# Second norm's rstd in two steps, another PSUM set for a bias product, later token blocks in a fused transformer block

## The chip, the cores and the metric

The kernel runs on one core of a Trainium2 chip. The core has a matrix engine (TensorE, PE in the profile), three engines for elementwise work (VectorE or DVE, ScalarE or ACT, GpSimd or POOL), a queue that issues transfers (SyncE or SP) and 16 DMA engines. Each engine takes its own instructions in the order in which they stand in its queue, and waits for others only where a semaphore says so. The metric is the time of one execution on the device, in microseconds (us).

## The reference

One residual layer on 512 tokens of width 2048, all in float32: a modulated norm, a projection shared by a recurrent and an attention group, an output projection, and then the part in which the change lies, a second modulated norm and a SwiGLU feed-forward of width 5632.

```python
x = x + gt1[:, None, :] * (mix @ w_out[l])

h2 = modulate(rms_norm(x, g_ffn[l]), sh2, sc2)
gate, up = jnp.split(h2 @ w_up[l], 2, axis=-1)
x = x + gt2[:, None, :] * ((jax.nn.silu(gate) * up) @ w_down[l])
```

`rms_norm` divides by the root of the mean square (rstd is its inverse) and multiplies by a gain; `modulate` multiplies by one plus a scale and adds a shift.

## The kernel before

Every product is made of three: each operand is split into a high part (written by ScalarE) and the low rest (written by VectorE), and high x high, high x low and low x high are summed in PSUM. A contraction of 2048 runs over 16 steps of 128 (k-steps). Activations lie transposed: features on partitions, 512 tokens along the free axis.

Weights come in raw pieces of 1 MB (tag `raw`, two buffers), and `stream` (from L188) splits each in two halves of 1024 columns (tags `whi` and `wlo`, three buffers each; L181 is the high part on ScalarE, L182 the low part on VectorE). One half serves two k-steps. `fm_group` (L201 on) computes four output blocks of 128 features at once, in four PSUM banks, 12 matmuls per k-step, and runs the functions in `hooks` after the k-steps that they are booked for.

The feed-forward goes in three stages:
- **Plain up groups** (`for gi in range(STD)`, L876 on): two groups, up0 and up1, of 16 k-steps. Their input `hr` is x times the gain of the norm, without rstd, since rstd of a token can be multiplied in later. The shift goes in as a bias product: `up_bias` sums shift x weight on VectorE into `bu_acc`, in 16 instructions, and a product with ones (`bup_p`, L886 to L888) adds it over the partitions; L889 copies it to `bup`. L892 to L895 then apply rstd, bias and SiLU.
- **Token side of the fast blocks.** For the other blocks of the up projection a Strassen-like scheme of seven half-size products is used. `make_t(j)`, j = 0 to 7, prepares its token-side operands from a pair of feature blocks: rstd and gain (`h2x`, L824), shift (L825), sums and differences (`ta`, `tb`) and splits (`tb`, `tc`, `td`, `te` with h and l). It is VectorE and ScalarE work and runs as hooks of up0 and up1: j = 0 to 3 after the k-steps 6, 9, 12, 15 of up0, j = 4 to 7 after the k-steps 0, 3, 6, 9 of up1. From j = 2 on its results go to pages (`t_tags`) that hold `hr` until up1 has used it, so they wait for k-steps of up1.
- **Fast blocks** uf4 to uf43 (from L931), and then the **down projection**: dn0 to dn3 in two passes.

rstd itself is made by `rstd_bcast`, booked after k-step 4 of up0 (`R1STEP`): four small matmuls add the squares (`rstd_1a`), VectorE copies four columns (`rstd_1t`), GpSimd raises to the power -1/2 (L232, L235), four matmuls spread the result over the partitions (`rstd_1b`), ScalarE copies it out.

PSUM has eight banks in two sets: `acc` is one set of four; `misc` (three) with `rgp` (one) is the other. `bank(i, f, name)` gives set `acc` for even i and the other for odd i. up0 has `acc`, up1 the other set; fast block f takes `bank(f + 1, ...)`, and down group g of pass pi `bank(g + pi, ...)`. A bank is free for the next user when its last reader has read it.

The order of each queue is set by a scheduler from the priority of each piece of code (its place in the program, moved by `high_priority`), within what data and buffers allow.

Of the kernel before, what the change touches and what calls it, by code (L numbers as in the profile page):

```python
# [60 lines left out]
def block_kernel(ctx, tc, xT, crow, adaT, vecs, bfr, w1, wyr, wqkv0, wqkv, wgate, wout, wup0, wups, wdown, outT):  # L61
# [19 lines left out]
    def misc(name):  # L81
        return psm.tile([P, S], F32, tag="misc", name=name, bufs=3)

    def rgp(name):
# [151 lines left out]
        if inv is not None:  # L236
            nc.gpsimd.tensor_mul(inv, inv, out)

    def rstd_bcast(ssq, n, name, inv=None, times=None):
        ps = rgp(name + "a")  # L240
        for t in range(NT):
            nc.tensor.matmul(ps[:, t:t + 1], lhsT=ssq[:, t * P:(t + 1) * P], rhs=ones[:, 0:1], start=True, stop=True)
        tok = small(NT, name + "t")
        nc.vector.tensor_copy(out=tok, in_=ps[:, :NT])
        rms_rstd(tok, tok, n, inv)
        if times is not None:
            nc.gpsimd.tensor_mul(tok, tok, times)
        pb = rgp(name + "b")
        for t in range(NT):
            nc.tensor.matmul(pb[:, t * P:(t + 1) * P], lhsT=tok[:, t:t + 1].broadcast_to([P, P]), rhs=ident,  # L250
                             start=True, stop=True)
        out = cp.tile([P, S], F32, name=name, tag="rstd_b", bufs=2)
        nc.scalar.activation(out, pb, AF.Copy)
        return out
# [496 lines left out]
    def bank(i, f, name):  # L751
        return acc(name) if i % 2 == 0 else (misc(name) if f < 3 else rgp(name))
# [120 lines left out]
        nc.sync.dma_start(out=d[1], in_=lo)  # L873
        actd.append(d)

    for gi in range(STD):  # L876
        hk = {}
        if gi == 0:
            add(hk, R1STEP, lambda: r1.append(rstd_bcast(ssq_1, D, "rstd_1")))
        for j in range(gi * 4, gi * 4 + 4):  # L880
# [1 line left out]
        bu_acc = cp.tile([P, S], F32, name=f"bu_acc{gi}", tag="rstd_b", bufs=2)
        bup = cp.tile([P, 4], F32, name=f"bup{gi}")
        ps = fm_group(wup0[gi], list(range(KT)), hr, f"up{gi}", hooks=hk, raw_hook=lambda q, raw: up_bias(q, raw, bu_acc),
                      ps=[bank(gi, f, f"up{gi}p{f}") for f in range(4)])
# [1 line left out]
        for f in range(4):
            nc.tensor.matmul(pb[:, f:f + 1], lhsT=bu_acc[:, f * P:(f + 1) * P], rhs=ones[:, 0:1], start=True, stop=True)  # L888
        nc.vector.tensor_copy(out=bup, in_=pb[:, :4])  # L889
        for f in range(2):  # L890
# [176 lines left out]
```

## Time and profile before

| | us |
|---|---|
| median of 3 runs | 2217.01 (2216.24 to 2224.03) |
| the profiled execution | 2219.23 |
| its span, first to last instruction | 2217.5 |
| PE busy in the span | 2114.4 (95%) |
| DVE busy | 1589.6 (72%) |
| ACT busy | 879.1 (40%) |
| mean granted TensorE clock | 0.981 of full |

The profile is of one execution. A timeline row gives the start, the duration, the engine, the line, and in square brackets how long the engine was idle before and what ended that. Durations of instructions that follow each other overlap a little, so work is summed from start to start where a stretch is full. The granted clock 1.0 is the level 2.4 GHz, 0.5 the level 1.2 GHz.

### The profile page before, as it was taken

Reading aid. Unit: us, or ns where it says so; the run is one execution under the profiler, and the core shown is the slowest. Engines: PE = TensorE matmul, PEld = TensorE weight load, DVE = VectorE, ACT = ScalarE, POOL = GpSimd, SP = SyncE. Lnnn points to the kernel's source line nnn. Section 1 sums busy time; section 2 is a strip of 40 time slices with the busy share of each in tenths; the row PEclk is TensorE's granted clock in tenths of the full one; section 3 lists DMA queues with packets and bytes.
Section 4 is the critical chain, followed back from the end, with each engine's and each line's share of the span. In section 5 each row is a group of like instructions: output and inputs, shape, how many; then the busy total and the mean of one; then the engine's idle time right before and its main releaser. Section 6 shows DMA issues by size and latency. Waiting matters only on the chain.

```text
span 2217.5 us, 32702 instructions
## 1 busy us (share of the span) xinstructions
PE 2114.4 (95%) x12785; PEld 1917.1 (86%) x12785; DVE 1589.6 (72%) x2407; ACT 879.1 (40%) x1238; POOL 217.8 (10%) x169
## 2 busy tenths in 40 slices
PE   8988988898989989899999999999999999999999
PEld 5768887887778878799999999999999888888887
DVE  8997678878877777988888888888888343322332
ACT  5522336657443334544444444444444222222111
POOL 2260113333112400000000000000000000000000
PEclk9999999999999999999999999999999999999999
DMA  9868565565657762343444344433444985554443
GB/s 315 319 208 294 190 230 195 194 235 190 233 179 268 261 221 77 114 133 125 128 139 133 125 128 140 133 125 128 139 133 139 325 296 192 175 199 140 158 156 110
DMA packets 133021, 406.05 MB, mean 183 GB/s; under 512 B 14561, under 2 KB 19841, under 8 KB 123138
## 3 DMA queue, kind: packets, MB, share of 16 engines
q1 hardware_dynamic: 132866, 403.96, 54.1%
q8 instruction: 100, 1.64, 0.3%
q14 instruction: 55, 0.45, 0.1%
HBM read 361.15 MB, written 42.75 MB: 182 GB/s over the span
## 4 chain that ended last, share of the span: by engine, by line
PE 66%; DVE 14%; DMA 12%; issue 4%; ACT 3%; POOL 1%; SPq 0%; POOLq 0%; DVEq 0%; ACTq 0%
PE dn_0p L186 5%; PE dn_3p L186 5%; PE dn_1p L186 5%; PE dn_2p L186 5%; DMA ada<-in_adaT 4%; DMA bw<-in_w 2%; DVE adf L143 2%; DVE ada L133 1%; PE up0p L186 1%; DVE ada L143 1%; PE yr1p L186 1%; DMA xrl<-xrd 1%; DMA adf<-in_adaT 1%; PE up1p L186 1%; PE uf42p L941 1%
## 5 line engine op out<-in xcount | busy, mean ns | idle before, releaser
L133 DVE SCALAR_TENSOR_TENSOR ada<-ada,c_b 128x1024 f32<-128x1024 f32 x128 | 167.3, 1319 | 53.5 <-DMA ada<-in_adaT 53.4
L182 DVE TENSOR_TENSOR uq_0tl<-uq_0r,uq_0th 128x1024 fp32r<-128x1024 f32 x40 | 49.0, 1225 | 63.6 <-ACT uq_0th L181 63.6
L181 ACT ACTIVATE uq_0sh<-uq_0r 128x1024 fp32r<-128x1024 f32 x40 | 42.5, 1062 | 89.5 <-PE uf5p L941 2.3
L182 DVE TENSOR_TENSOR uq_0al<-uq_0r,uq_0ah 128x1024 fp32r<-128x1024 f32 x40 | 49.0, 1225 | 40.0 <-ACT uq_0ah L181 40.0
L181 ACT ACTIVATE uq_1th<-uq_1ra 128x1024 fp32r<-128x1024 f32 x40 | 42.5, 1061 | 73.0 <-DVE uq_1ra L921 3.0
L181 ACT ACTIVATE uq_0th<-uq_0r 128x1024 fp32r<-128x1024 f32 x40 | 42.4, 1060 | 72.4 <-DVE uq_0r L921 1.9
L181 ACT ACTIVATE uq_1sh<-uq_1rb 128x1024 fp32r<-128x1024 f32 x40 | 42.5, 1062 | 70.3 <-PE uf43p L941 2.4
L181 ACT ACTIVATE uq_1ah<-uq_1ra 128x1024 fp32r<-128x1024 f32 x40 | 42.5, 1062 | 60.7 <-issue 59.1
L181 ACT ACTIVATE uq_0ah<-uq_0r 128x1024 fp32r<-128x1024 f32 x40 | 42.4, 1060 | 51.7 <-issue 48.1
L143 DVE SCALAR_TENSOR_TENSOR adf<-adf,c_b 128x1024 f32<-128x1024 f32 x32 | 56.5, 1765 | 2.7 <-DMA adf<-in_adaT 2.7
L182 DVE TENSOR_TENSOR uq_1tl<-uq_1ra,uq_1th 128x1024 fp32r<-128x1024 f32 x40 | 49.0, 1226 | 10.5 <-ACT uq_1th L181 10.4
L186 PE MATMUL w1p<-hph,w1h 128*128 128x512 f32 x128 | 48.3, 405 | 7.7 <-ACT hph L315 7.6
L186 PE MATMUL w1p<-hpl,w1h 128*128 128x512 f32 x128 | 51.7, 404 | 2.3 <-DVE hpl L316 2.2
L182 DVE TENSOR_TENSOR uq_0sl<-uq_0r,uq_0sh 128x1024 fp32r<-128x1024 f32 x40 | 49.0, 1226 | 3.7
L182 DVE TENSOR_TENSOR uq_1sl<-uq_1rb,uq_1sh 128x1024 fp32r<-128x1024 f32 x40 | 49.0, 1226 | 2.7 <-ACT uq_1sh L181 0.6
L186 PE MATMUL w1p<-hph,w1l 128*128 128x512 f32 x128 | 50.5, 394 | 0.0
L182 DVE TENSOR_TENSOR uq_1al<-uq_1ra,uq_1ah 128x1024 fp32r<-128x1024 f32 x40 | 48.6, 1215 | 0.1
L562 DVE SCALAR_TENSOR_TENSOR ba<-bw,sh,ba 128x512 f32<-128x512 f32 x45 | 33.5, 756 | 19.4 <-DMA bw<-in_w 17.0
L143 DVE SCALAR_TENSOR_TENSOR ada<-ada,c_b 128x1024 f32<-128x1024 f32 x32 | 41.2, 1288 | 3.6 <-DMA ada<-in_adaT 3.6
L182 DVE TENSOR_TENSOR dn_1l<-dn_2r,dn_1h 128x1024 fp32r<-128x1024 f32 x11 | 13.5, 1226 | 38.2 <-ACT dn_1h L181 38.2
L182 DVE TENSOR_TENSOR dn_0l<-dn_2r,dn_0h 128x1024 fp32r<-128x1024 f32 x11 | 13.5, 1225 | 37.6 <-ACT dn_0h L181 37.6
L182 DVE TENSOR_TENSOR dn_1l<-dn_0r,dn_1h 128x1024 fp32r<-128x1024 f32 x11 | 13.5, 1225 | 37.0 <-ACT dn_1h L181 37.0
(13854 smaller groups left out, 8429.3 us busy)
## 6 DMA issues: line engine op xcount, KB each, us to landing
ada<-in_adaT SPq DMA_DIRECT2D x160, 512.0 KB, 5.1
uq_0r<-in_wups SPq DMA_DIRECT2D x80, 512.0 KB, 4.1
uq_1ra<-in_wups SPq DMA_DIRECT2D x40, 512.0 KB, 4.0
uq_1rb<-in_wups SPq DMA_DIRECT2D x40, 512.0 KB, 3.3
adf<-in_adaT SPq DMA_DIRECT2D x32, 512.0 KB, 5.4
actd<-ach SPq DMA_DIRECT2D x44, 256.0 KB, 2.1
actd<-acl SPq DMA_DIRECT2D x44, 256.0 KB, 4.0
dn_0r<-in_wdown SPq DMA_DIRECT2D x11, 1024.0 KB, 5.0
```

The source lines that it names most:

```text
L133: nc.vector.scalar_tensor_tensor(out=t, in0=t, scalar=1.0, in1=cs, op0=ALU.mult, op1=ALU.mult, accum_out=ac)
L143: nc.vector.scalar_tensor_tensor(out=t, in0=t, scalar=1.0, in1=c_b[:, cs], op0=ALU.mult, op1=ALU.mult, accum_out=ada_acc[j][:, hf, i:i + 1])
L181: nc.scalar.activation(R(hi[:, :n]), raw_ap, AF.Copy)
L182: tail_lo.append(nc.vector.tensor_sub(R(lo[:, :n]), raw_ap, hi[:, :n]).ins)
L186: nc.tensor.matmul(ps, lhsT=R(l), rhs=R(r), start=start, stop=stop)
L562: nc.vector.scalar_tensor_tensor(out=ba[j], in0=src, scalar=s1, in1=ba[j], op0=ALU.mult, op1=ALU.add)
L941: nc.tensor.matmul(m[p], lhsT=R(w[:, ks]), rhs=R(x), start=first and p in opens, stop=last, skip_group_check=True)
```

## The change

Four things. (1) `rstd_bcast` is cut into `sums` and `spread`: for the second norm the sums are booked after k-step 7 of up0 and the spreading after k-step 9, in place of both after k-step 4. (2) `make_t` is booked after the k-steps 10, 11, 13, 15 of up0 and 0, 4, 9, 15 of up1 (`T_STEPS`). (3) The bias product of up1 goes to a bank of set `acc`, and its copy gets a higher priority; up0's stays in `misc`. (4) The fast block f takes `bank(f, ...)` in place of `bank(f + 1, ...)`, so that uf4 has `acc` and uf43 the other set. The number of instructions is the same.

```diff
-R1STEP = 4
+R1STEP = (7, 9)
+T_STEPS = ((10, 11, 13, 15), (0, 4, 9, 15))
...
-    def rstd_bcast(ssq, n, name, inv=None, times=None):
-        ps = rgp(name + "a")
+    def rstd_parts(ssq, n, name, inv=None, times=None):
+
         tok = small(NT, name + "t")
...
+        def sums():
+            ps = rgp(name + "a")
...
+        def spread():
+            pb = rgp(name + "b")
...
+    def up_fin(gi, ps, bu_acc):
+        bup = cp.tile([P, 4], F32, name=f"bup{gi}")
+        pb = acc(f"bup_p{gi}") if gi % 2 else misc(f"bup_p{gi}")
+        for f in range(4):
+            nc.tensor.matmul(pb[:, f:f + 1], lhsT=bu_acc[:, f * P:(f + 1) * P], rhs=ones[:, 0:1], start=True, stop=True)
+        with tc.high_priority(offset=600):
+            nc.vector.tensor_copy(out=bup, in_=pb[:, :4])
+        up_out(gi, ps, bup, range(2))
...
-            add(hk, R1STEP, lambda: r1.append(rstd_bcast(ssq_1, D, "rstd_1")))
-        for j in range(gi * 4, gi * 4 + 4):
-            add(hk, (R1STEP + 2 if gi == 0 else 0) + (j % 4) * 3, lambda j=j: make_t(j))
+            r1_sums, r1_spread = rstd_parts(ssq_1, D, "rstd_1")
+            add(hk, R1STEP[0], r1_sums)
+            add(hk, R1STEP[1], lambda: r1.append(r1_spread()))
+        for j in range(4):
+            add(hk, T_STEPS[gi][j], lambda j=j + 4 * gi: make_t(j))
...
-        pb = misc(f"bup_p{gi}")
...
-        ps = [bank(f + 1, b, f"uf{f}p{b}") for b in range(4)]
+        ps = [bank(f, b, f"uf{f}p{b}") for b in range(4)]
```

What this does to the queues stands in the order of the built programs, at three places. First PE in up0, around the rstd of the second norm. Before, at the end of k-step 4:

```order
L186 MATMUL up0p_7046<-hrh_6969,up_0l 128x512
L242 MATMUL rstd_1a<-ones,ssq_5686 128x1 x4
L186 MATMUL up0p_7043<-hrh_6973,up_0h 128x512
L186 MATMUL up0p_7043<-hrl_6974,up_0h 128x512
L186 MATMUL up0p_7043<-hrh_6973,up_0l 128x512
L250 MATMUL rstd_1b<-ident,rstd_1t 128x128 x4
L186 MATMUL up0p_7044<-hrh_6973,up_0h 128x512
```

After, at the end of k-step 7, with 24 matmuls of two k-steps between the two products:

```order
L187 MATMUL up0p_7046<-hrh_6981,up_1l 128x512
L247 MATMUL rstd_1a<-ones,ssq_5686 128x1 x4
L187 MATMUL up0p_7043<-hrh_6985,up_0h 128x512
...
L187 MATMUL up0p_7046<-hrh_6989,up_0l 128x512
L256 MATMUL rstd_1b<-ident,rstd_1t 128x128 x4
L187 MATMUL up0p_7043<-hrh_6993,up_1h 128x512
```

So the spreading stands 24 matmuls behind the sums, where it stood three behind. Next DVE at the same place, where `rstd_1t` is the copy between the two products and `up0r` a raw piece of weights. Before:

```order
L770 SCALAR_TENSOR_TENSOR hrl_7038<-x_15_7029,a_5685,hrh_7037 128x512
L182 TENSOR_TENSOR up_0l<-up0r_7219,up_0h 128x1024
L863 SCALAR_TENSOR_TENSOR bu_acc_7041<-up0r_7219,mod_118,bu_acc_7041 128x512
L244 COPY rstd_1t<-rstd_1a 128x4
L863 SCALAR_TENSOR_TENSOR bu_acc_7041<-up0r_7219,mod_118,bu_acc_7041 128x512
L863 SCALAR_TENSOR_TENSOR bu_acc_7041<-up0r_7311,mod_118,bu_acc_7041 128x512 x2
L824 SCALAR_TENSOR_TENSOR h2x_7175<-x_0_6038,a_5685,rstd_7145 128x512
L824 SCALAR_TENSOR_TENSOR h2x_7180<-x_1_6041,a_5685,rstd_7145 128x512
L863 SCALAR_TENSOR_TENSOR bu_acc_7041<-up0r_7311,mod_118,bu_acc_7041 128x512
```

After:

```order
L183 TENSOR_TENSOR up_0l<-up0r_7179,up_0h 128x1024
L875 SCALAR_TENSOR_TENSOR bu_acc_7042<-up0r_7179,mod_118,bu_acc_7042 128x512 x2
L875 SCALAR_TENSOR_TENSOR bu_acc_7042<-up0r_7310,mod_118,bu_acc_7042 128x512 x4
L183 TENSOR_TENSOR up_1l<-up0r_7179,up_1h 128x1024
L248 COPY rstd_1t<-rstd_1a 128x4
L183 TENSOR_TENSOR up_0l<-up0r_7310,up_0h 128x1024
L183 TENSOR_TENSOR up_1l<-up0r_7310,up_1h 128x1024
L836 SCALAR_TENSOR_TENSOR h2x_7236<-x_0_6038,a_5685,rstd_7218 128x512
L836 SCALAR_TENSOR_TENSOR h2x_7241<-x_1_6041,a_5685,rstd_7218 128x512
```

The copy now stands behind the sums of the last raw piece (up0r_7310) and one more split, and two more splits stand between it and the first `h2x`. Then DVE at the end of up1, where uq are weights of the first fast block and bup the bias. Before:

```order
L863 SCALAR_TENSOR_TENSOR bu_acc_7467<-up1r_7783,mod_118,bu_acc_7467 128x512 x2
L182 TENSOR_TENSOR uq_0al<-uq_0r,uq_0ah 128x1024
...
L833 TENSOR_TENSOR tc7l<-h2x_7730,tc7h 128x512
L842 TENSOR_TENSOR tb_7736<-ta_7735,h2x_7730 128x256
L833 TENSOR_TENSOR td7l<-ta_7735,td7h 128x512
L892 TENSOR_TENSOR sg_0_7851<-up1p_7469,rstd_7145 128x512
L833 TENSOR_TENSOR te7l<-tb_7736,te7h 128x512
L889 COPY bup_7468<-bup_p_7845 128x4
L894 TENSOR_TENSOR su_0_7852<-up1p_7471,rstd_7145 128x512
```

After:

```order
L875 SCALAR_TENSOR_TENSOR bu_acc_7467<-up1r_7752,mod_118,bu_acc_7467 128x512
L836 SCALAR_TENSOR_TENSOR h2x_7814<-x_14_7017,a_5685,rstd_7218 128x512
L903 COPY bup_7844<-bup_p_7845 128x4
L836 SCALAR_TENSOR_TENSOR h2x_7819<-x_15_7029,a_5685,rstd_7218 128x512
...
L854 TENSOR_TENSOR tb_7825<-ta_7824,h2x_7819 128x256
L845 TENSOR_TENSOR td7l<-ta_7824,td7h 128x512
L891 TENSOR_TENSOR sg_0_7851<-up1p_7468,rstd_7218 128x512
L845 TENSOR_TENSOR te7l<-tb_7825,te7h 128x512
L893 TENSOR_TENSOR su_0_7852<-up1p_7470,rstd_7218 128x512
L891 TENSOR_TENSOR sg_1_7864<-up1p_7469,rstd_7218 128x512
```

The copy of the bias moved from behind the last token block (`te7l`) to the first `h2x` behind the last sum of `bu_acc`. Last, PE at the start of the down projection, where dn_0p_17573 to 17576 are the four banks. Before:

```order
L941 MATMUL uf43p_17239<-tc7h,uq_1tl 128x256
L186 MATMUL dn_0p_17573<-adh_17477,dn_00_0h 128x512
L186 MATMUL dn_0p_17573<-adl_17478,dn_00_0h 128x512
L186 MATMUL dn_0p_17573<-adh_17477,dn_00_0l 128x512
L186 MATMUL dn_0p_17573<-adh_17481,dn_00_0h 128x512
L186 MATMUL dn_0p_17573<-adl_17482,dn_00_0h 128x512
...
L186 MATMUL dn_0p_17573<-adl_17490,dn_00_1h 128x512
L186 MATMUL dn_0p_17574<-adh_17477,dn_00_0h 128x512
L186 MATMUL dn_0p_17574<-adl_17478,dn_00_0h 128x512
L186 MATMUL dn_0p_17574<-adh_17477,dn_00_0l 128x512
```

After:

```order
L962 MATMUL uf43p_17239<-tc7h,uq_1tl 128x256
L187 MATMUL dn_0p_17573<-adh_17477,dn_00_0h 128x512
L187 MATMUL dn_0p_17573<-adl_17478,dn_00_0h 128x512
L187 MATMUL dn_0p_17573<-adh_17477,dn_00_0l 128x512
L187 MATMUL dn_0p_17574<-adh_17477,dn_00_0h 128x512
L187 MATMUL dn_0p_17574<-adl_17478,dn_00_0h 128x512
L187 MATMUL dn_0p_17574<-adh_17477,dn_00_0l 128x512
L187 MATMUL dn_0p_17575<-adh_17477,dn_00_0h 128x512
```

Before, the first bank takes 11 matmuls by itself until the next is used; after, the banks take turns from the first k-step on.

## Rows read from the trace of the kernel before

**Rows 1.** Head of the page and its first part: the span, then busy time, share and instructions of each engine.
```profile
span 2217.5 us, 32702 instructions
PE 2114.4 (95%) x12785; PEld 1917.1 (86%) x12785; DVE 1589.6 (72%) x2407; ACT 879.1 (40%) x1238; POOL 217.8 (10%) x169
```
**Rows 2.** Busy time of each engine by stretches: the stretch in us, its length, then PE, PEld, DVE, ACT, POOL busy (instructions), the granted clock, DMA share, GB/s. In order: the rstd in up0; from the first `h2x` to the bias copy of up0; from that copy to the last token block; from the bias product of up1 to the middle of uf4; the first 11 matmuls of the down projection.
```profile
822.90:838.30 15.40, 8.40 (x31) 6.35 (x30) 12.35 (x19) 3.92 (x7) 2.21 (x2) 0.67 0.27 96
835.25:866.55 31.30, 31.30 (x137) 25.90 (x136) 20.01 (x33) 14.08 (x20) 0.00 (x0) 0.95 0.19 68
866.55:917.95 51.40, 44.17 (x196) 36.35 (x195) 50.74 (x87) 29.46 (x46) 0.00 (x0) 0.96 0.29 103
...
917.40:928.80 11.40, 10.20 (x58) 9.73 (x58) 9.93 (x17) 5.30 (x8) 0.00 (x0) 0.72 0.25 92
...
1732.50:1736.70 4.20, 4.20 (x12) 3.29 (x13) 3.40 (x9) 1.26 (x2) 0.00 (x0) 0.59 1.01 385
```
**Rows 3.** PE in order of time, around the rstd of the second norm in up0: the first matmul of up0, the last before the sums, the sums, the spreading.
```profile
809.56 0.39 PE L186 MATMUL up0p<-hrh,up_0h 128*128 128x512 f32 x1
...
822.93 0.39 PE L186 MATMUL up0p<-hrh,up_0l 128*128 128x512 f32 x1
826.96 1.05 PE L242 MATMUL rstd_1a<-ones,ssq 128*128 128x1 f32 x8 [3.64 <-DVE ssq L262]
...
832.53 2.08 PE L250 MATMUL rstd_1b<-ident,rstd_1t 128*128 128x128 f32 x8 [3.36 <-POOL rstd_1t L235]
```
**Rows 4.** PE, the same spreading for the first norm, early in the program.
```profile
116.49 1.16 PE L250 MATMUL rstd_xb<-ident,rstd_xt 128*128 128x128 f32 x8 [1.69 <-POOL rstd_xt L235]
```
**Rows 5.** DVE in order of time, from the rstd copy to the bias copy of up0.
```profile
829.28 0.75 DVE L863 SCALAR_TENSOR_TENSOR bu_acc<-up0r,mod,bu_acc 128x512 f32<-128x512 f32 x1
829.94 0.16 DVE L244 COPY rstd_1t<-rstd_1a 128x4 f32<-128x4 f32 x1
830.06 2.33 DVE L863 SCALAR_TENSOR_TENSOR bu_acc<-up0r,mod,bu_acc 128x512 f32<-128x512 f32 x3
835.28 1.41 DVE L824 SCALAR_TENSOR_TENSOR h2x<-x,a,rstd 128x512 f32<-128x512 f32 x2 [2.89 <-ACT rstd L253]
...
861.25 1.23 DVE L182 TENSOR_TENSOR up_1l<-up1r,up_1h 128x1024 fp32r<-128x1024 f32 x1 [4.21 <-ACT up_1h L181]
866.60 0.16 DVE L889 COPY bup<-bup_p 128x4 f32<-128x4 f32 x1 [4.13 <-PE bup_p L888]
```
**Rows 6.** SP in order of time: the issue of the last raw piece of up0.
```profile
823.61 0.33 SPq L192 DMA_DIRECT2D up0r<-in_wup  x1
```
**Rows 7.** The chain of waits: a transfer of an earlier raw piece of up0, from issue to landing.
```profile
804.40 5.60 DMA up0r<-in_wup
```
**Rows 8.** PE in order of time, from the bias product of up1 into uf4.
```profile
917.43 1.87 PE L888 MATMUL bup_p<-ones,bu_acc 128*128 128x1 f32 x8 [7.23 <-DVE sg L892]
919.64 0.55 PE L941 MATMUL uf4p<-tb0h,uq_0ah 128*128 128x256 f32 x1 [0.35 <-DVE bup L889]
...
924.43 0.28 PE L941 MATMUL uf4p<-te0h,uq_0ch 128*128 128x256 f32 x1
...
927.19 0.28 PE L941 MATMUL uf4p<-te7h,uq_1cl 128*128 128x256 f32 x1
...
928.84 0.39 PE L941 MATMUL uf4p<-td0h,uq_0sl 128*128 128x256 f32 x1 [0.76 <-DVE uq_0sl L182]
```
**Rows 9.** DVE in order of time at the end of up1: the last sums of `bu_acc`, the read of up1's first bank, the last token block, the bias copy, two splits of uf4's weights.
```profile
909.41 1.54 DVE L863 SCALAR_TENSOR_TENSOR bu_acc<-up1r,mod,bu_acc 128x512 f32<-128x512 f32 x2
...
916.69 0.68 DVE L892 TENSOR_TENSOR sg<-up1p,rstd 128x512 f32<-128x512 f32 x1
917.29 0.68 DVE L833 TENSOR_TENSOR te7l<-tb,te7h 128x512 fp32r<-128x512 f32 x1
919.33 0.16 DVE L889 COPY bup<-bup_p 128x4 f32<-128x4 f32 x1 [1.36 <-PE bup_p L888]
...
923.33 0.69 DVE L916 TENSOR_TENSOR uq_0cl<-uq_0r,uq_0ch 128x512 fp32r<-128x512 f32 x1
...
927.56 1.23 DVE L182 TENSOR_TENSOR uq_0sl<-uq_0r,uq_0sh 128x1024 fp32r<-128x1024 f32 x1
```
**Rows 10.** PE in order of time at the start of the down projection: the last matmul of uf43, the first and the twelfth of dn0.
```profile
1729.22 0.28 PE L941 MATMUL uf43p<-tc7h,uq_1tl 128*128 128x256 f32 x1
1732.50 0.51 PE L186 MATMUL dn_0p<-adh,dn_0h 128*128 128x512 f32 x1 [3.00 <-issue]
...
1736.68 0.39 PE L186 MATMUL dn_0p<-adh,dn_0h 128*128 128x512 f32 x1
```
**Rows 11.** DVE in order of time at the same place: its two reads of uf43's first bank.
```profile
1731.65 0.42 DVE L946 TENSOR_TENSOR ug<-uf43p,uw 128x256 f32<-128x256 f32 x1
1731.98 0.41 DVE L947 TENSOR_TENSOR uw<-uf43p,uw 128x256 f32<-128x256 f32 x1
```
**Rows 12.** PE in order of time: two waits elsewhere.
```profile
228.16 0.63 PE L404 MATMUL pc<-lf,triu 128*128 128x32 f32 x2 [2.65 <-DVE lf L402]
...
410.02 0.44 PE L186 MATMUL h5p<-h_0h,hh 128*128 128x384 f32 x1 [1.71 <-DVE vl L437]
```
**Rows 13.** Busy time by stretches (columns as in rows 2): the stretches behind the two waits.
```profile
228.00:236.00 8.00, 7.84 (x32) 7.76 (x33) 4.55 (x14) 0.69 (x1) 0.00 (x0) 0.60 0.63 229
410.00:418.00 8.00, 7.98 (x43) 7.46 (x44) 7.81 (x14) 5.55 (x12) 4.07 (x3) 1.00 0.47 151
```

More of the change, by code (lines that the diff above doesn't have):

```diff
@@ L237, in rms_rstd, with rstd_bcast @@
             nc.gpsimd.tensor_mul(inv, inv, out)
-    def rstd_bcast(ssq, n, name, inv=None, times=None):
-        ps = rgp(name + "a")
-        for t in range(NT):
-            nc.tensor.matmul(ps[:, t:t + 1], lhsT=ssq[:, t * P:(t + 1) * P], rhs=ones[:, 0:1], start=True, stop=True)
+    def rstd_parts(ssq, n, name, inv=None, times=None):
         tok = small(NT, name + "t")
[L244 to L254, printed above, removed]
+        def sums():
+            ps = rgp(name + "a")
+            for t in range(NT):
+                nc.tensor.matmul(ps[:, t:t + 1], lhsT=ssq[:, t * P:(t + 1) * P], rhs=ones[:, 0:1], start=True, stop=True)
+            nc.vector.tensor_copy(out=tok, in_=ps[:, :NT])
+            rms_rstd(tok, tok, n, inv)
+            if times is not None:
+                nc.gpsimd.tensor_mul(tok, tok, times)
+        def spread():
+            pb = rgp(name + "b")
+            for t in range(NT):
+                nc.tensor.matmul(pb[:, t * P:(t + 1) * P], lhsT=tok[:, t:t + 1].broadcast_to([P, P]), rhs=ident,
+                                 start=True, stop=True)
+            out = cp.tile([P, S], F32, name=name, tag="rstd_b", bufs=2)
+            nc.scalar.activation(out, pb, AF.Copy)
+            return out
+        return sums, spread
+    def rstd_bcast(*a, **kw):
+        sums, spread = rstd_parts(*a, **kw)
+        sums()
+        return spread()
     def square_acc(ssq, src, first, name, tag, eng=None):
@@ L874, in spill_act, with up_out @@
         actd.append(d)
-    for gi in range(STD):
-        hk = {}
-        if gi == 0:
-            add(hk, R1STEP, lambda: r1.append(rstd_bcast(ssq_1, D, "rstd_1")))
-        for j in range(gi * 4, gi * 4 + 4):
-            add(hk, (R1STEP + 2 if gi == 0 else 0) + (j % 4) * 3, lambda j=j: make_t(j))
[L882 to L885, printed above, removed]
-        pb = misc(f"bup_p{gi}")
[L887 to L890, printed above, removed]
+    def up_out(gi, ps, bup, fs):
+        for f in fs:
             t, t2 = page(f"sg{gi}_{f}", "d"), page(f"su{gi}_{f}", "d")
@@ L896, in block_kernel @@
             spill_act(t, 2 * gi + f)
+    def up_fin(gi, ps, bu_acc):
[6 more added lines that the diff above has]
+        up_out(gi, ps, bup, range(2))
+    for gi in range(STD):
+        hk = {}
+        if gi == 0:
+            r1_sums, r1_spread = rstd_parts(ssq_1, D, "rstd_1")
[3 more added lines that the diff above has]
+            add(hk, T_STEPS[gi][j], lambda j=j + 4 * gi: make_t(j))
+        bu_acc = cp.tile([P, S], F32, name=f"bu_acc{gi}", tag="rstd_b", bufs=2)
+        ps = fm_group(wup0[gi], list(range(KT)), hr, f"up{gi}", hooks=hk, raw_hook=lambda q, raw: up_bias(q, raw, bu_acc),
+                      ps=[bank(gi, f, f"up{gi}p{f}") for f in range(4)])
+        up_fin(gi, ps, bu_acc)
     def fast_chunk(f, c):
```

## The prediction

> **What bounds the kernel now.** I read the head of the page first, then the busy times by stretch, then PE's and VectorE's rows in order of time. PE is busy for 95% of the span [rows 1], so time can be won only where PE waits, or runs at the low clock after a wait. Three stalls stand where the change touches: in up0 PE waits 3.64 us for the last sum of squares and, three matmuls later, 3.36 us for rstd [rows 3], and the granted clock over that stretch is 0.67 [rows 2]; at the end of up1 it waits 7.23 us for a VectorE row and then goes into uf4 at 0.72 [rows 8, 2]; at the start of the down projection it stands still for 3.00 us and runs its first 11 matmuls at 0.59 [rows 10, 2]. Last I read VectorE between the first two: from the bias copy of up0 to the last token block it is busy for 50.74 of 51.40 us [rows 2]. There it is the bound, and PE's 7.23 us are its lead. Before that copy it has room: 20.01 us of work in 31.30 [rows 2], with 4.21 and 4.13 us of idle time in one piece each, since the copy waits for PE to end up0 [rows 5].
>
> **The rstd in two steps.** The 60 matmuls before the sums start 0.227 us apart (822.93 less 809.56, by 59) [rows 3], so up0's 192 take 43.5 us at the full clock, and a k-step of 12 takes 2.72. After, the sums stand behind k-step 7, at 809.56 + 8 x 2.72 = 831.3. The last square was added before PE's 826.96, so that wait is gone. The copy on VectorE is now behind six sums of 0.66 (829.28 to 829.94) and a split of 1.13, so at 829.28 + 4.0 + 1.1 = 834.4 [rows 5]; from copy to spreading took 832.53 - 829.94 = 2.6 us [rows 3, 5], which makes 837.0. PE gets there at 809.56 + 10 x 2.72 + 1.05 for the sums = 837.8. The second wait is gone too, by 0.8 us, and with both the low clock. The spreading took 2.08 us at the low clock and 1.16 for the first norm [rows 3, 4]; I take 1.16. The bias product of up0 I take at 0.95, half of the 1.87 of its sister at the low clock [rows 8]. So PE lets the copy go at 809.56 + 43.5 + 1.05 + 1.16 + 0.95 = 856.2, where it went at 866.60.
>
> **Is VectorE there by then?** The first `h2x` came 2.75 us after the spreading began, 0.67 after its end [rows 3, 5]: now 837.8 + 1.16 + 0.67 = 839.6, which is 4.3 later than before. What stands from there to the copy is the same list less three splits (1.23), two sums (0.75) and one difference of 256 columns, priced as the 0.42 of a 256-column row [rows 11]: 20.01 - 5.6 = 14.4 us. That gives 854.0 without any wait; with all of the small waits on ScalarE that were there (31.30 - 20.01 - 4.21 - 4.13 = 2.95) it gives 857.0. PE's 856.2 lies between; I take 856.4. **First term: 866.60 - 856.4 = 10.2 us.**
>
> **From the copy to uf4.** The later bookings of `make_t` change the order within this stretch and not the work: from the bias copy of up0 to `uq_0cl` VectorE has 96 instructions for 95, one difference more, 0.34. The pages for the token blocks come free with k-steps of up1, which move with the copy. So the stretch keeps its length. At its end the bias copy of up1 no longer waits for a product that itself waited for a bank of up1: 1.36 us of VectorE's idle time go [rows 9]. In its place the copy waits for a product that starts with the last sum of `bu_acc`, with one `h2x` (0.66) between: 0.4 us at the full clock, 1.3 at the low one; I take 0.5, since PE's wait is short there (below). Net -1.36 + 0.34 + 0.5 = **second term: 0.5 us**, so `uq_0cl` starts at 923.33 - 10.7 = 912.6 [rows 9].
>
> What becomes of PE's 7.23 us? up1 ends at 910.20 (917.43 less the wait) and now 10.4 earlier, at 899.8. The last sum ended at 910.95 [rows 9]; it is 10.2 earlier but stands 1.4 us further back (behind a split and a small row), so 902.1: PE waits 2.3 us in place of 7.23. Then 24 matmuls of uf4, 0.12 apart at the full clock (927.19 less 924.43, by 23) or 4.8 us in all as before [rows 8], bring it to 906 or 908, and there it waits for `uq_0cl` until 913.3. So most of the wait is not removed; it moves behind the bias product. After it come 22 matmuls at the low clock, some 4.4 us, while VectorE needs 4.8 from the end of `uq_0cl` to that of `uq_0sl` [rows 9], on which PE waited before as well. That covers nearly all; I charge 0.4 for matmuls still slow behind it. **Third term: -0.4 us.** PE passes `uq_0sl` at 928.84 - 10.3 = 918.5, and from there each fast block is PE's alone, before and after.
>
> What that second part costs by a page is told apart from the sum. A wait of 1.71 us was followed by a clock of 1.00 and one of 2.65 by 0.60 [rows 12, 13]; 2.3 lies between, so the bias product may run at either level. The Trainium skill, TensorE: Matmul & The Clock Gate, section HAM oscillation, tells of a kernel in which each wait between bursts of matmuls brings the low clock back, once per burst, so that two waits cost more than one. By it the change buys a second fall of the clock: the bias product takes 1.87, the copy waits 1.3, and the sum below would be 0.8 less. By the shorter of the two rows it is nothing. The sum keeps the 0.5.
>
> **The other set for the fast blocks.** uf43 had the banks that dn0 wants first. dn0's first matmul starts 0.11 us after VectorE's second read of uf43's first bank ends (1731.98 + 0.41 = 1732.39) [rows 10, 11]; the profile names no releaser ("issue"), so the bank is my inference. Now uf43 has the other set, and dn0's banks are those of uf42, read while uf43 runs. The weights' first half was split before uf43 ended, and the operands of dn0's first k-steps were loaded while it ran. So the idle time from 1729.34 to 1732.50 goes, 3.16 us, and the 11 slow matmuls take 11 x 0.227 = 2.5 in place of 1736.68 - 1732.50 = 4.18. **Fourth term: 3.16 + 1.7 = 4.8 us.** If the bank was not the cause, it is 0. At the start of uf4 the new set costs nothing: up0's banks are read long before, and the bias product's own bank, which uf4 wants last, is free with the copy.
>
> **The sum** is 10.2 + 0.5 - 0.4 + 4.8 = 15.1 us. The profiled execution took 2219.23 (span 2217.5), so 2204.1; it was 2.2 above the median of the runs shown. On the median's scale: 2217.01 - 15.1 = **2201.9**.
>
> **Rivals.**
> - *VectorE is late at the first copy.* ScalarE's high parts of weight splits wait for PE, and what token work stands behind them in its queue waits as well; one such wait was 4.21 us on VectorE [rows 5]. One of that size left in the stretch puts the copy at 860.6 and the time at 2201.9 + 4.2 = 2206.1. For it: the stretch is now nearly full. Against: PE passes the buffers sooner. Chance 0.14.
> - *The bank is not what dn0 waits for*, and the change of sets does nothing: 2201.9 + 4.8 = 2206.7. For it: the releaser is not named. Against: the 0.11 us. Chance 0.12.
> - *PE is let go sooner.* If ScalarE and VectorE close up so that the wait on `uq_0cl` shrinks from 5 us to nothing: about 2197. Against: VectorE is full. Chance 0.06.
> - *Slower.* The copy of the sums is now queued behind four sums that read the last raw piece. Issued at 823.61, and 5.60 us on the way as an earlier one [rows 6, 7], it lands at 829.2, and VectorE wants it at 830.6; with the 0.8 of slack at the spreading, 2.2 us are free. Every further microsecond holds PE at the spreading. It loses the whole gain if it lands 17.3 us late, 22.9 after issue: slower than before beyond that. Nothing in that stretch loads the queues so (DMA share 0.27) [rows 2]. Chance 0.03.
>
> **How the numbers follow.** My forecast has 0.65, its own range 2199 to 2205. A run of this kernel can tell about 0.5% from no change, which is 11.1 us, so faster means below 2205.9. Nearly all of the forecast lies there (0.62), half of the late VectorE (0.07) and the early PE (0.06): 0.75 faster. The rest of the first and the bank's rival make 0.22 for no change, and 0.03 is left for slower. The range reaches down to 2197.5, most of the third rival, and up to 2208, past the second: 0.1 to 0.15 is left out.
>
> **What would show it.** Right: no wait of PE at the sums and the spreading, the first bias copy near 856, a short wait before the second bias product and a longer one inside uf4 before `uq_0cl`, VectorE without a gap between, and dn0's first matmul 0.12 us after uf43's last. Wrong: a wait of PE at the spreading (raw piece late), VectorE idle between 840 and 856, or dn0 still some 3 us behind uf43.

## The result, and the profile after

The changed kernel took 2205.08 us (median of 6 runs, 2202.41 to 2208.44), the kernel before 2218.48 beside it (6 runs, 2216.24 to 2225.72). The ratio is 0.9933 with a 95% interval of 0.9912 to 0.9954: 14.9 us less, between 10.2 and 19.5 (it is not the ratio of the two medians, which lie 13.4 apart). The profiled execution of the changed kernel took 2206.86 us.

Head of the page and its first part for the changed kernel, columns as in [rows 1]:

```profile
span 2205.1 us, 32703 instructions
PE 2108.9 (96%) x12785; PEld 1915.9 (87%) x12785; DVE 1590.6 (72%) x2407; ACT 879.4 (40%) x1238; POOL 222.6 (10%) x169
```

The span is 12.4 us shorter and VectorE has as much work as before. PE's busy time fell by 5.5 us without one matmul less, since fewer of them run at the low clock.

Before any row is laid beside one of before, the zero has to be moved. PE in order of time, the first matmul of up0, the sums and the spreading:

```profile
812.73 0.39 PE L187 MATMUL up0p<-hrh,up_0h 128*128 128x512 f32 x1
...
834.49 0.94 PE L247 MATMUL rstd_1a<-ones,ssq 128*128 128x1 f32 x8
...
840.96 1.16 PE L256 MATMUL rstd_1b<-ident,rstd_1t 128*128 128x128 f32 x8
```

up0 starts 3.17 us later than in [rows 3], though the queues ahead of it are the same. An experiment below shows that this start moves by 11 us between executions. So from here a place in the program is given as **its start less the start of up0's first matmul**, which takes that spread out.

Neither product of the rstd waits any more; [rows 3] had 3.64 and 3.36 us there. DVE in order of time, from the rstd copy to the first bias copy:

```profile
838.47 0.15 DVE L248 COPY rstd_1t<-rstd_1a 128x4 f32<-128x4 f32 x1
838.54 1.22 DVE L183 TENSOR_TENSOR up_0l<-up0r,up_0h 128x1024 fp32r<-128x1024 f32 x1
841.95 1.23 DVE L183 TENSOR_TENSOR up_1l<-up0r,up_1h 128x1024 fp32r<-128x1024 f32 x1 [2.20 <-ACT up_1h L182]
843.09 1.41 DVE L836 SCALAR_TENSOR_TENSOR h2x<-x,a,rstd 128x512 f32<-128x512 f32 x2
...
859.30 0.16 DVE L903 COPY bup<-bup_p 128x4 f32<-128x4 f32 x1 [0.54 <-PE bup_p L901]
```

The first `h2x` comes at 30.4 (843.09 less 812.73; 25.7 before), the bias copy at 46.6 (57.0 before), and it waits 0.54 us for PE in place of 4.13: PE and VectorE end the stretch together. Busy times by stretches, columns as in [rows 2]: the rstd in up0, from the bias copy to the last token block, a stretch inside uf4, and the first 11 matmuls of the down projection.

```profile
822.90:838.30 15.40, 15.40 (x73) 12.86 (x72) 15.13 (x21) 5.69 (x8) 0.00 (x0) 1.00 0.43 153
...
859.25:911.20 51.95, 47.68 (x225) 39.66 (x224) 51.15 (x90) 30.27 (x47) 0.00 (x0) 1.00 0.29 102
...
913.75:921.50 7.75, 6.52 (x29) 6.22 (x30) 7.35 (x12) 3.32 (x5) 0.00 (x0) 0.50 0.36 135
...
1721.70:1724.20 2.50, 2.50 (x13) 2.08 (x12) 1.32 (x2) 1.33 (x2) 0.00 (x0) 1.00 0.81 276
```

The granted clock of the rstd stretch went from 0.67 to 1.00, that of the down projection's start from 0.59 to 1.00. VectorE is as full behind the bias copy as before. But inside uf4 there are now 7.75 us at 0.50, the level 1.2 GHz. PE in order of time says why, from the second bias product on:

```profile
905.00 1.05 PE L901 MATMUL bup_p<-ones,bu_acc 128*128 128x1 f32 x8 [2.10 <-DVE bu_acc L875]
905.92 0.36 PE L962 MATMUL uf4p<-tb0h,uq_0ah 128*128 128x256 f32 x1
...
908.75 0.28 PE L962 MATMUL uf4p<-tc3h,uq_0al 128*128 128x256 f32 x1
913.79 0.58 PE L962 MATMUL uf4p<-te0h,uq_0ch 128*128 128x256 f32 x1 [4.76 <-ACT uq_0ch L936]
...
915.78 0.58 PE L962 MATMUL uf4p<-te0h,uq_0cl 128*128 128x256 f32 x1 [1.19 <-DVE uq_0cl L937]
...
920.64 0.41 PE L962 MATMUL uf5p<-te0h,uq_0ch 128*128 128x256 f32 x1
...
921.49 0.35 PE L962 MATMUL uf4p<-td0h,uq_0sl 128*128 128x256 f32 x1
```

The 7.23 us of [rows 8] became 2.10 in front of the bias product and 4.76 + 1.19 inside uf4: 8.05 us, where [rows 8] have 8.34 with the 0.35 and 0.76 that follow the 7.23. `uq_0sl`, on which PE waited before, no longer holds it; slow matmuls do (0.21 us apart at 917 to 921). VectorE and ScalarE in the same place, for [rows 9]:

```profile
904.20 0.75 DVE L875 SCALAR_TENSOR_TENSOR bu_acc<-up1r,mod,bu_acc 128x512 f32<-128x512 f32 x1
...
906.09 0.16 DVE L903 COPY bup<-bup_p 128x4 f32<-128x4 f32 x1 [0.48 <-PE bup_p L901]
...
912.32 0.74 DVE L894 SCALAR_TENSOR_TENSOR sg<-su,bup,sg 128x512 f32<-128x512 f32 x1
...
915.04 0.69 DVE L937 TENSOR_TENSOR uq_0cl<-uq_0r,uq_0ch 128x512 fp32r<-128x512 f32 x1
```
```profile
912.50 0.72 ACT L892 ACTIVATE sg<-sg,bup 128x512 f32<-128x512 f32 x1 [1.14 <-DVE sg L891]
913.13 0.61 ACT L936 ACTIVATE uq_0ch<-uq_0r 128x512 fp32r<-128x512 f32 x1
```

ScalarE has idle time before `sg` and none before `uq_0ch`, so `uq_0ch` was held by what stands ahead of it, the outputs of up1. PE at the start of the down projection, for [rows 10], and VectorE's reads of uf43's first bank, for [rows 11]:

```profile
1721.59 0.28 PE L962 MATMUL uf43p<-tc7h,uq_1tl 128*128 128x256 f32 x1
1721.71 0.40 PE L187 MATMUL dn_0p<-adh,dn_0h 128*128 128x512 f32 x1
...
1724.23 0.39 PE L187 MATMUL dn_0p<-adh,dn_0l 128*128 128x512 f32 x1
```
```profile
1724.03 0.42 DVE L967 TENSOR_TENSOR ug<-uf43p,uw 128x256 f32<-128x256 f32 x1
1724.36 0.41 DVE L968 TENSOR_TENSOR uw<-uf43p,uw 128x256 f32<-128x256 f32 x1
```

dn0 starts 0.12 us behind uf43's last matmul, and its first 11 matmuls are over before VectorE has read uf43's first bank.

All ten profiles by places, each counted from up0's first matmul. The fourth column is the matmul with which PE gets past `uq_0sl` [rows 8]. It does not have the same work ahead of it in every kernel: 51 matmuls of uf4 before and in "rstd alone", 39 in "outputs later", 49 in "outputs last", 51 and two of uf5 in the others.

| kernel | start of up0 | first bias copy | uq_0cl on DVE | td0h x uq_0sl on PE | dn0's 12th matmul | end of span |
|---|---|---|---|---|---|---|
| before | 809.56 | 57.04 | 113.77 | 119.28 | 927.12 | 1407.94 |
| changed | 812.73 | 46.57 | 102.31 | 108.76 | 911.50 | 1392.37 |
| changed, again | 801.39 | 46.38 | 102.26 | 108.55 | 911.22 | 1392.01 |
| set alone | 812.83 | 57.56 | 114.28 | 120.24 | 923.01 | 1403.87 |
| rstd alone | 811.35 | 46.38 | 103.32 | 109.03 | 916.39 | 1397.75 |
| rstd in one step | 805.53 | 56.22 | 111.37 | 117.33 | 920.10 | 1400.97 |
| rstd at k-step 8 | 801.15 | 48.52 | 104.52 | 110.98 | 913.73 | 1394.55 |
| early blocks | 806.61 | 47.07 | 103.95 | 110.14 | 912.82 | 1393.69 |
| outputs later | 804.32 | 46.46 | 96.11 | 101.34 | 907.39 | 1388.18 |
| outputs last | 811.36 | 46.66 | 96.33 | 101.64 | 904.89 | 1385.74 |

From up0 on, the change is worth 15.6 us by the first profile (1407.94 less 1392.37) and 15.9 by the second.

### The profile page after: what moved, and what is told of

It reads as the page before. It is cut to its first block, busy times and chain, and to the rows that moved or that the text cites. A ratio compares the mean times of both kernels' runs of the same rounds, so it can differ in the third digit from the quotient of the medians.

```text
span 2205.1 us, 32703 instructions
## 1 busy us (share of the span) xinstructions
PE 2108.9 (96%) x12785; PEld 1915.9 (87%) x12785; DVE 1590.6 (72%) x2407; ACT 879.4 (40%) x1238; POOL 222.6 (10%) x169
## 4 chain that ended last, share of the span: by engine, by line
PE 73%; DVE 12%; DMA 8%; ACT 3%; issue 2%; POOL 1%; SPq 0%; DVEq 0%; POOLq 0%; ACTq 0%
PE dn_0p L187 5%; PE dn_3p L187 5%; PE dn_2p L187 5%; PE dn_1p L187 5%; DMA ada<-in_adaT 2%; PE up0p L187 2%; PE wo2p L187 2%; PE wo3p L187 2%; PE wo1p L187 2%; DMA bw<-in_w 2%; DVE adf L144 2%; DVE ada L144 1%; PE uf5p L962 1%; PE uf42p L962 1%; PE uf35p L962 1%
## 5 line engine op out<-in xcount | busy, mean ns | idle before, releaser
L182 ACT ACTIVATE uq_0ah<-uq_0r 128x1024 fp32r<-128x1024 f32 x40 | 42.4, 1060 | 50.4 <-issue 46.8
```

What stands on the lines that cost most here:

```text
L182: nc.scalar.activation(R(hi[:, :n]), raw_ap, AF.Copy)
```

## The experiments

The set alone, the rstd alone, the rstd in one step and the outputs behind the first half of weights shared one chip (the kernel before: 2218.71 us there), the other four another (2217.19).

**The changed kernel again.** No edit.

> The changed kernel once more, without an edit. In the profiles so far up0's first matmul comes 804.3 to 812.8 us after the start, though the queues ahead of it are the same. Theory A: that spread is one of the executions, so in this run up0 may start anywhere in it, while all that follows repeats to 0.3 us: first bias copy 46.6 us after up0's first matmul, td0h x uq_0sl 108.8, dn0's first matmul 909.0, end of the span 1392.4. Rival G: the start of up0 is fixed by the built program; it comes at 812.7 +- 1 again.

Measured: 2200.08 us, ratio 0.9928 (0.9908 to 0.9949). up0 starts at 801.39, 11.3 us earlier than in the first profile, and each place behind it repeats to 0.4 us, where I had 0.3. Theory A holds, the rival is out. The two executions part step by step from 174 to 650 us, in the part of the program ahead of the feed-forward (0.1 us apart at the spreading of the first norm, 1.6 at the first product `h0p`, 7.3 at `h7p`, 14.9 at `ratioa`, 11.3 at up0). So the times of a few runs can't weigh a term of 1 or 2 us here; the places from up0 on can.

**The bank set alone.** The kernel before with

```diff
-        ps = [bank(f + 1, b, f"uf{f}p{b}") for b in range(4)]
+        ps = [bank(f, b, f"uf{f}p{b}") for b in range(4)]
```

> The kernel before with one edit: fast block f takes the bank set of f in place of f + 1. Theory A (dn0's first matmul waited for VectorE's reads of uf43's first bank, as the fourth term has it): dn0 starts 0.12 us behind uf43's last matmul in place of 3.3, its first 11 matmuls run at the full clock (2.5 us in place of 4.2), and the time falls by 4.8 us, to about 2213.7 against 2218.5; the rstd stall in up0 and the 7.23 us wait in front of the second bias product stay. Rival B (dn0 waited for something else, weights or an operand, which the changed kernel reaches earlier because the stretch ahead is shorter): dn0 still stands some 3 us and the time stays within 1 us.

Measured: 2213.82 us, ratio 0.9982 (0.9969 to 0.9995). PE in order of time at the start of the down projection:

```profile
1733.20 0.28 PE L941 MATMUL uf43p<-tc7h,uq_1tl 128*128 128x256 f32 x1
1733.32 0.40 PE L186 MATMUL dn_0p<-adh,dn_0h 128*128 128x512 f32 x1
...
1735.84 0.39 PE L186 MATMUL dn_0p<-adh,dn_0l 128*128 128x512 f32 x1
```

From uf43's last matmul to dn0's twelfth it is 2.64 us, 7.46 before: 4.82 less, with nothing else changed ahead of the down projection but the set. The bank it was; rival B is out. The wait in front of the bias product does not stay as I had written: it is 2.65 in place of 7.23, since uf4's first matmuls, no longer in want of up1's banks, now stand ahead of it in PE's queue. The stretch got no shorter by that: uq_0sl is passed 0.96 us later, of which 0.52 stood at the first bias copy already, ahead of the fast blocks.

**The rstd and the bookings alone.** The changed kernel with both bank edits and the priority taken back. In the code the priority stands ahead of the copies of both groups, up0's too, so it goes for both:

```diff
-        pb = acc(f"bup_p{gi}") if gi % 2 else misc(f"bup_p{gi}")
+        pb = misc(f"bup_p{gi}")
...
-        with tc.high_priority(offset=600):
-            nc.vector.tensor_copy(out=bup, in_=pb[:, :4])
+        nc.vector.tensor_copy(out=bup, in_=pb[:, :4])
...
-        ps = [bank(f, b, f"uf{f}p{b}") for b in range(4)]
+        ps = [bank(f + 1, b, f"uf{f}p{b}") for b in range(4)]
```

> The changed kernel with the bank edits taken back: fast block f has the set of f + 1, and the second bias product is in the old set again, its copy without the higher priority. The rstd in two steps and the later bookings stay. Theory A: the first bias copy keeps its place, 46.6 us after up0's first matmul (57.0 before), PE waits in front of the second bias product as before (about 7 us, less what it now gains), uf4 passes uq_0sl some 10 us earlier than before, dn0 stands about 3 us again: about 10.5 us below the kernel before, 2208. Rival C (the bank of the bias product matters by itself, since the wait in front of it and the wait in uf4 add up): uf4 passes uq_0sl 2 us or more later than in the changed kernel, so that the time is 2210 or more.

Measured: 2210.44 us, ratio 0.9950 (0.9931 to 0.9969). PE in order of time:

```profile
908.16 1.86 PE L901 MATMUL bup_p<-ones,bu_acc 128*128 128x1 f32 x8 [6.83 <-DVE sg L891]
...
1720.74 0.28 PE L961 MATMUL uf43p<-tc7h,uq_1tl 128*128 128x256 f32 x1
1724.02 0.47 PE L187 MATMUL dn_0p<-adh,dn_0h 128*128 128x512 f32 x1 [3.00 <-issue]
```

The bias copy keeps its 46.4, the waits of 6.83 and 3.00 are back, and uq_0sl is passed at 109.0, 0.3 to 0.5 behind the changed kernel: theory A. Rival C had 2 us or more there; its time, 2210 or more, is met by the median, but from up0 on this kernel ends 10.2 us below the one before, where theory A had 10.5. By the times the two halves add up, 4.0 us (1.1 to 6.9) for the set and 11.1 (6.9 to 15.3) for the rest against 14.9 for the whole, but these intervals are too wide to show it. By the places they don't quite: 4.1 and 10.2 make 14.3, where the whole change has 15.6 and 15.9. Of what is missing, 0.5 is the late first copy of the set alone; about 1 us comes only with both halves, on VectorE, as "Earlier token blocks" shows.

**The rstd in one step again.** The changed kernel with

```diff
-R1STEP = (7, 9)
+R1STEP = (4, 4)
```

> The changed kernel with one edit: both halves of the rstd stand behind k-step 4 again. Theory A (the first term is PE's two waits and the low clock behind them, 10.2 us): PE waits some 3.6 us at the sums and 3.4 at the spreading, the first bias copy is back at about 57 us after up0's first matmul in place of 46.6, and the time is about 10 us over the changed kernel, 2215. Rival D (VectorE was the bound of the stretch and the later token blocks gave it the room): the copy comes at 52 or earlier and half of the gain stays, 2210 or less.

Measured: 2209.40 us, ratio 0.9959 (0.9946 to 0.9973). PE and then DVE in order of time:

```profile
823.52 1.87 PE L247 MATMUL rstd_1a<-ones,ssq 128*128 128x1 f32 x8 [4.23 <-DVE ssq L274]
...
829.09 1.22 PE L256 MATMUL rstd_1b<-ident,rstd_1t 128*128 128x128 f32 x4 [2.21 <-POOL rstd_1t L236]
```
```profile
861.75 0.16 DVE L903 COPY bup<-bup_p 128x4 f32<-128x4 f32 x1 [4.13 <-PE bup_p L901]
```

The waits come back, the copy goes from 46.5 to 56.2 and waits 4.13 for PE as it did before: PE was the bound, not VectorE. By the median alone rival D's 2210 would have passed; its up0 started at 805.53, and from up0 on the end is 8.8 us later than in the mean of the two profiles of the changed kernel. Theory A holds with 8.8 at the end for 9.7 at the copy.

**The spreading at k-step 8.** The changed kernel with

```diff
-R1STEP = (7, 9)
+R1STEP = (7, 8)
```

> The changed kernel with one edit: the spreading of rstd stands behind k-step 8 in place of 9, 12 matmuls (2.72 us) earlier on PE. In the changed kernel GpSimd ended rstd at 840.91 and PE took it up at 840.96, so there is no slack. Theory A (what comes late there is paid by PE one for one, and the low clock on top): PE waits about 2.7 us at the spreading, the first bias copy moves from 46.6 to 49.3 or, with the low clock, up to 50.5 us after up0's first matmul, and the time rises by 2.7 to 4. Rival D (VectorE sets the end of the stretch, its token blocks start with rstd): the first h2x comes at the same time or 1.1 us earlier, the copy stays within 0.5 us, and so does the time.

Measured: 2205.25 us, ratio 0.9959 (0.9941 to 0.9978); from up0 on 2.4 us over the changed kernel. PE, then DVE, in order of time:

```profile
828.63 1.16 PE L256 MATMUL rstd_1b<-ident,rstd_1t 128*128 128x128 f32 x8 [1.88 <-POOL rstd_1t L236]
...
895.69 1.87 PE L901 MATMUL bup_p<-ones,bu_acc 128*128 128x1 f32 x8 [2.42 <-DVE bu_acc L875]
```
```profile
830.45 1.42 DVE L836 SCALAR_TENSOR_TENSOR h2x<-x,a,rstd 128x512 f32<-128x512 f32 x2 [3.03 <-ACT rstd L259]
...
849.67 0.16 DVE L903 COPY bup<-bup_p 128x4 f32<-128x4 f32 x1 [2.29 <-PE bup_p L901]
```

Asked for 2.72 us sooner, rstd makes PE wait 1.88, so in this execution 0.84 were free behind k-step 9. The copy comes 2.0 later, with the first `h2x` 1.1 earlier (29.3 against 30.4): theory A by its mechanism, a little under its 2.7. Rival D is out again.

**Earlier token blocks.** The changed kernel with

```diff
-T_STEPS = ((10, 11, 13, 15), (0, 4, 9, 15))
+T_STEPS = ((10, 12, 14, 15), (0, 3, 6, 9))
```

> The changed kernel with one edit: the token blocks are booked behind the k-steps 10, 12, 14, 15 of up0 and 0, 3, 6, 9 of up1, as near to the old bookings as the later rstd allows. Theory A (the bookings change the order and not the work, and VectorE has no gap to fill): copy, uq_0cl and uq_0sl keep their places within 0.5 us, and so does the time. Rival H (the later bookings let up1's weight splits and bias sums go first, so without them PE waits in up1 or the second bias product comes later): uf4 passes uq_0sl 1.5 us or more later.

Measured: 2199.86 us, ratio 0.9929 (0.9910 to 0.9948); from up0 on 1.3 to 1.7 us over the changed kernel, uq_0sl passed 1.4 to 1.6 later. PE, then DVE, in order of time:

```profile
835.34 1.16 PE L256 MATMUL rstd_1b<-ident,rstd_1t 128*128 128x128 f32 x8 [0.42 <-POOL rstd_1t L236]
```
```profile
899.47 0.16 DVE L903 COPY bup<-bup_p 128x4 f32<-128x4 f32 x1 [0.81 <-PE bup_p L901]
...
903.22 0.43 DVE L852 TENSOR_TENSOR tb<-h2x,h2x 128x256 f32<-128x256 f32 x1 [0.85 <-ACT h2x L837]
```

Theory A's half microsecond is passed, and rival H has the size but not its reason: PE waits 1.10 in front of the bias product, less than the 2.10 of the changed kernel. 0.42 is lost at the rstd; the rest is VectorE, which waits 0.81 and 0.85 behind the last sum of `bu_acc`, where the changed kernel has one wait of 0.48. VectorE's way from the first copy to `uq_0cl` tells the same: 56.73 us before, 56.72 with the set alone, 56.94 with the later bookings alone, 56.88 with the new bank and nearly the old bookings, but 55.74 and 55.88 with both, and 55.15 and 56.00 with both in the two runs that move the rstd. By these profiles, one of each kernel but the changed one, neither edit is worth anything here by itself. The new bank of the bias product and the priority of its copy were not tried apart.

**The outputs of up1 behind uf4's first half of weights, and behind all of uf4's products.** The changed kernel, where `up_fin` now hands the call back, with

```diff
-        up_out(gi, ps, bup, range(2))
+        return lambda: up_out(gi, ps, bup, range(2))
...
-            for p, hi, lo in fast_chunk(f, c):
+            ops = fast_chunk(f, c)
+            if f == 2 * STD and c == 0:
+                late()
+            for p, hi, lo in ops:
```

and, in the second, `late()` behind the loop over both chunks of uf4. For up0 the call stays where it was.

> The changed kernel with one edit: the outputs of up1 (rstd, SiLU, product, split: 8 VectorE rows) are written behind the first half of uf4's weights, so that uq_0ch and uq_0cl no longer wait for pages that these outputs hold. Theory A (most of PE's 7.23 us was only moved into uf4, 4.76 for uq_0ch and 1.19 for uq_0cl, with about 36 matmuls at the low clock behind them): the wait shrinks to about 2 us, uf4 passes uq_0sl some 5 us sooner, and the time falls by about 5 us more, to 2200. Rival E (VectorE is the bound right through uf4, so work put off only comes back as a later wait, for uq_1cl, for uq_0tl or for uf5's banks): the time stays within 1.5 us of the changed kernel.

> As the run with up1's outputs behind the first half of uf4's weights, but with these outputs behind all of uf4's products. Theory A (it is the pages and VectorE's order in front of uq_0cl that cost, and they are out of the way already): within 1.5 us of that run, about 4 us below the changed kernel when both are counted from up0's first matmul. Rival E (what is put off comes back): the outputs of up1 are then read so late that uf5 waits for up1's banks or for pages, and the time is 2 us or more above that run.

Measured: 2194.63 us, ratio 0.9889 (0.9877 to 0.9902), and 2196.52 us, ratio 0.9915 (0.9896 to 0.9933). From up0 on they are 4.0 and 6.4 us under the changed kernel (mean of its two profiles, 1392.2). PE of the first and DVE of the second in order of time, then stretches of the second (columns as in [rows 2]):

```profile
904.40 0.39 PE L967 MATMUL uf4p<-td0h,uq_0sh 128*128 128x256 f32 x1 [1.00 <-ACT uq_0sh L182]
...
905.66 0.39 PE L967 MATMUL uf4p<-td0h,uq_0sl 128*128 128x256 f32 x1 [0.76 <-DVE uq_0sl L183]
```
```profile
907.69 0.69 DVE L939 TENSOR_TENSOR uq_0cl<-uq_0r,uq_0ch 128x512 fp32r<-128x512 f32 x1
...
917.55 0.69 DVE L891 TENSOR_TENSOR sg<-up1p,rstd 128x512 f32<-128x512 f32 x1
```
```profile
904.60:907.50 2.90, 2.90 (x26) 2.90 (x25) 2.58 (x7) 2.76 (x6) 0.00 (x0) 1.00 0.85 277
907.50:913.00 5.50, 4.02 (x28) 3.13 (x26) 5.50 (x10) 2.91 (x5) 0.00 (x0) 1.00 0.11 45
```

`uq_0cl` comes 6 us sooner (96.1 and 96.3), the wait of 4.76 is gone, and in the second the clock stays at 1.00 through uf4. So what the change moved into uf4 was a real cost and could be had: it was the place of up1's outputs ahead of uf4's weights, in the pages or in the queues (the two runs don't part these), and not a lack of engine time. Rival E had less than 1.5 us of gain for the first and 2 us of loss for the second, and is out by that; no wait of PE stands behind uf4. A little of it is true of the first, which passes `uq_0sl` 7.2 to 7.4 us sooner and keeps 4.0: 14 matmuls that stood ahead of that place now stand behind it (1.7 us), and 1.6 us go in short stops of PE between 915.7 and 919.3, the longest a wait of 0.69 for `uq_1th`. Theory A had the second within 1.5 us of the first and 4 us under the changed kernel, which was too little. Both versions are below the kernel before. Below the changed kernel the first is by its ratio as well, while the interval of the second (0.9896 to 0.9933) overlaps that of the changed kernel on the same chip (0.9908 to 0.9949), so there the gain is shown by the places alone. By the places the second is the better by 2.4 us; their medians lie the other way round, with starts of up0 at 804.32 and 811.36 in the profiles, so the runs don't settle which is.

## Why the prediction came out right, step by step

Forecast 2201.9 with a gain of 15.1; measured a gain of 14.9 by the ratio, and 15.6 and 15.9 from up0 on. The changed kernel's own median was 2205.1 on one occasion and 2200.1 on the other. The first median lies 0.1 outside the forecast's own range, 2199 to 2205, but it belongs to a kernel before of 2218.48 and not of 2217.01; on the forecast's scale the ratio gives 2217.01 x 0.9933 = 2202.2. The two spans differ by only 12.4 us because up0 started 3.2 us later in the profiled execution of the changed kernel, which I had not reckoned with.

- **First term, 10.2 us:** 10.5 and 10.7 at the copy (57.04 less 46.57 and 46.38). Undoing it alone moved the copy by 9.7. The working holds in its parts: PE waits at neither product, the copy was forecast at 46.8 and VectorE got there as PE did. Shown, by that experiment and the one with k-step 8, that PE's waits and their clock were the cause. Too large was the slack at the spreading: I had 0.8 us; GpSimd ended rstd 0.05 us before PE took it up in the first profile, 0.84 were free in another, and with the early blocks PE waited 0.42. What took it is VectorE's copy of the sums, which came at 25.7 (838.47 less 812.73) where I had 24.8 (834.4 less 809.56). That the little left was enough is luck.
- **Second term, 0.5 us:** 0.9 to 1.0. From copy to `uq_0cl` the stretch went from 56.73 to 55.74 and 55.88. The copy of up1's bias waits 0.48 in place of 1.36, as forecast. The step that was mis-sized is that the later bookings change the order "and not the work", and cost 0.34 for one difference more: the stretch got no longer by it. By the runs the order is needed for the gain as much as the bank is.
- **Third term, -0.4 us:** -0.8 to -0.9 (from `uq_0cl` to td0h x uq_0sl 6.45 and 6.29 us, 5.51 before). The mechanism is the one forecast: 2.10 us of wait before the product (2.3), then 4.76 + 1.19 in uf4 and slow matmuls behind. Two matmuls of uf5 now stand ahead of that place and took 0.43 us, so half of the term is only order, and uf43 has 0.3 back.
- **The page on the clock.** In the first profile the wait of 2.10 us left the bias product at 1.05 us and uf4 at the full level until the wait of 4.76, so by this trace the second fall of the clock, which the Trainium skill (TensorE: Matmul & The Clock Gate, section HAM oscillation) would have put there, did not come. In the second profile of the same kernel it did, after a wait of 2.24 and a product of 1.05: from 896.2, 1.7 us into uf4, the matmuls start 0.21 apart (rows in the last section). It cost nothing there: the slow matmuls ran in the time of the wait for `uq_0ch`, which was 3.63 in place of 4.76 and ended at the same place (101.0 and 101.1). With the spreading at k-step 8 the fall came at once: a wait of 2.42, a product of 1.87, and a bias copy that waited 1.29 in place of 0.48. That is the 0.8 us that I had set beside the sum; but the stretch to `uq_0cl` took 56.00 there against 55.74 and 55.88, so at most 0.3 of it arrived.
- **Fourth term, 4.8 us:** 4.8 (7.46 less 2.64), and by the set alone 4.82. The inferred bank is shown to be the cause, though the profile names only "issue". The Trainium skill, PSUM — Partial Sum Buffer, section PSUM bank collisions raise a hardware error, has engines guarded from each other in PSUM by bank (or bank and quadrant of partitions) and not by address. The trace fits: dn0 stood until VectorE's second read of that bank was over. It cannot tell the two apart, since dn0's 512 columns fill the whole bank.
- **The sum.** The second and third terms were off by about half a microsecond each, in opposite directions, and the 0.3 in uf43 was in no term. That the total came so near, 15.6 and 15.9 for 15.1, is in that part luck; the two large terms came out each by itself, and each was taken back in a run of its own.
- **The rivals.** VectorE late at the first copy: one wait of the kind was there, 2.20 us before the first `h2x`, and none else as long, and the copy came where I had it; not borne out. The bank not the cause: out. PE let go sooner: not by this change, but the last two experiments make it so, at 4.0 and 6.4 us, where I had 5. Slower by a late raw piece: VectorE's six sums of 832.73 to 837.4 ran without a gap, so the piece had landed; a later landing was not tried.

## What to carry to other kernels

A wait that sits in front of an engine's bound need not go when its named cause goes; look for what that engine meets next, and what holds that: here it was outputs that nobody needed yet, and moving them was worth another 4 to 6 us. Where two stages share banks, count which set the last user of one and the first of the next fall on: an idle time that a profile gives to "issue" was worth 4.8 us by one index. When the program ahead of the change spreads by more than the change is worth, count places from a mark just ahead of it.

## What I had not expected of the hardware

Ten profiles with the same queues ahead of up0 reach it between 801.15 and 812.83 us after the start. And the waits before the second bias product left PE at different clocks, without order by their length. After 2.09, 2.10 and 2.40 us the first 24 matmuls of uf4 start 0.12 us apart from the second on, the full level. After 2.42 the low level came at once (a product of 1.87), after 1.10 ("early blocks") 0.3 us into uf4, after 2.07 ("outputs later") 0.8 us and after 2.24 ("changed, again") 1.7 us into it. The last two, PE in order of time:

```profile
898.04 0.28 PE L967 MATMUL uf4p<-tb0h,uq_0al 128*128 128x256 f32 x1
...
898.52 0.42 PE L967 MATMUL uf4p<-tb2h,uq_0al 128*128 128x256 f32 x1
```
```profile
893.61 1.05 PE L901 MATMUL bup_p<-ones,bu_acc 128*128 128x1 f32 x8 [2.24 <-DVE bu_acc L875]
...
896.43 0.42 PE L962 MATMUL uf4p<-tc0h,uq_0al 128*128 128x256 f32 x1
...
902.40 0.39 PE L962 MATMUL uf4p<-te0h,uq_0ch 128*128 128x256 f32 x1 [3.63 <-ACT uq_0ch L936]
```

Two executions of the same kernel, with 2.10 and 2.24, differ in this. The length of the wait alone does not tell which it will be.
